# HGRN operands stored crosswise, and the modulation matmuls taken out of the attention stretch of a two-layer trunk kernel

## The chip, the cores and the metric

The kernel runs on one core of one Trainium2 chip. The metric is device time in microseconds (us) of one execution. It was run three times: 2095.54, 2097.5 and 2103.86 us, median 2097.5.

## The reference, cut to what matters

A step of a trunk of two layers (`DEPTH = 2`) over 512 latent and 128 context tokens, width 1024. Each layer makes six modulation vectors, `silu(c) @ w_mod[l] + b_mod[l]`, split as shift, scale and gate for the mixers (numbers 0, 1, 2) and for the FFN (3, 4, 5). One input projection feeds three mixers that run side by side: differential attention, a gated DeltaNet and HGRN2. An output projection, a gated residual with layer norm, a modulated SwiGLU FFN and a second norm follow.

HGRN2 is the part whose code changes:

```python
def gla_chunked(q, k, v, g, s0):          # per direction, scan over tokens
    attn = einsum('bhntsd,bhnsd->bhnts', q[..., :, None, :] * dec, k)   # dec = exp of summed log forget
    intra = einsum('bhnts,bhnse->bhnte', attn, v)
    ...
        o = intra_n + einsum('bhcd,bhde->bhce', qd_n, S)
        S = S * gl_n[..., None] + einsum('bhcd,bhce->bhde', kd_n, v_n)
```

It runs forwards and backwards over four heads of 64, with key = 1 - forget, and the two directions share q and v.

## The kernel before, in words

Tokens are handled in five tiles of 128 (`NT`, number `LT = 4` is the context). Float32 weights are split in two float32r parts: `raw_unit` (L251) loads up to 512 KB into one of three buffers `raw` (pool `praw`), `unit` (L266) lets ACT round them and DVE subtract, and PE multiplies in three passes. All loads and most stores are issued in order on SP's queue. The Tile framework orders each engine's instructions itself, by the order of the program text and a timeline of its own (`schedule_with_timeline_sim=True`, L1767).

A layer runs in these stages.

- First projections: `proj_bg` (L1265, psum tile `pbg`), then four `proj_B` blocks (L1247, `pbq`). `gate_out` (L1240) lets ACT and POOL make a gate and stores it (`gsc`) from a single buffer. In layer 0 they run from 42 to about 95 us, in layer 1 from 1053 to about 1115 us, there beside the norm of layer 0's end (`ptf`).
- The delta mixer, interleaved by `run` (L1332) with the other projections, up to about 350 and 1374 us.
- The attention stretch, up to about 524 and 1551 us. `run` takes turns: one attention query tile (L1187), then, once the delta is over (`open_h`, L1432), two draws of `mods` (L1387), one draw of `hgrn` (L690) and one of `delta_T`. `mods` makes the vectors 3, 4 and 2, folds the first norm's weights into 4 and 3 (`affine`, L506, through the DRAM tile `modrow`), and in layer 0 makes vector 1 of layer 1.
- Output projection (`pop`), with two draws of `mods_late` (L1395) in each of the last five steps: vector 5, and in layer 0 vector 0 of layer 1. Then the FFN (`pfa`, `pfb`, `pfc`, `pfd`, `pfo`); after its first part `affine` folds vectors 1 and 0 of layer 1 (L1677).

`modulation` (L466) takes for each vector eight raw tiles; each is multiplied by four matmuls of 32 columns into psum tile `psm` (the profile shows two records for a float32 matmul, so 8 records a tile). DVE adds the bias (`ms`), and two loads and two stores per vector go over SP. It yields four times per vector.

`hgrn_local` (L579) works with direction 0 on partitions 0 to 63 and direction 1 on 64 to 127. For each token tile, `hq` holds q for both directions, `hK` the keys, `hf` the forget gates. The opening (L605) makes keys on DVE, multiplies keys and queries on PE, masks the diagonal into `haD` on DVE and multiplies q by f on POOL. Then seven levels n = 1, 2, ..., 64 follow, with one draw each for all five tiles. Below 64, in each direction the blocks of the one parity act as queries and of the other as keys: ACT copies the active query blocks of both directions into a tile with zeros elsewhere (`hqm`, L623), eight matmuls of 128 rows by 64 columns per tile (`diag`, L596) sum both directions over all 128 partitions, and DVE puts the product into `haD` where the mask of the level says so (L624). The zeros keep the other direction out. At n = 64 the product goes to `hf` by ACT. At every level, DVE scales the query blocks of each direction (L646) and POOL the key blocks (L647) by gate products `hT`, which POOL makes in a tree (L650). At the end `key_T` (L654) transposes the keys for the states (`pha`), and `out` (L697) makes outputs.

```python
up, lo = 1 - d, d                                    # L640, in a loop over both directions
tt(V, half(Q, d, up), half(Q, d, up), tb(lo), ALU.mult)
tt(G, half(Kr, d, lo), half(Kr, d, lo), tb(up), ALU.mult)
```

PSUM has eight banks: pairs P1, P2, Q and R. `psum_phase` deals them out: first projections `g=QQ+RR`; in the attention stretch one bank (R1) for modulation and three (P2, P2b, R2) for HGRN.

## Time and profile before

| what | value |
|---|---|
| runs | 2095.54, 2097.5, 2103.86 us |
| profiled execution, its own time | 2094.8 us |
| span of that execution, first to last instruction | 2093.0 us |
| mean granted TensorE clock | 0.956 |
| bytes moved by DMA | 249.36 MB |

The profile is of one execution. Engines: PE is TensorE's matmuls, PEld its weight loads, DVE is VectorE, ACT is ScalarE, POOL is GpSimd, SP issues DMAs. A row names line, engine, operation, `written tile<-read tiles`, shape and count. Most instructions are recorded through helpers (L173 for matmuls, L176 for tensor_tensor), so they are told apart by tile names. Matmuls are pipelined: what a run of them costs is read from the start of one run to the start of the next, not from busy time alone.

### The profile page before, as it was taken

To read this page: it belongs to the slowest core of one execution; us is meant where nothing else is said; L and a number is where in the kernel's file an instruction comes from. 1 tells how busy PE (TensorE), PEld (TensorE's weight loads), DVE (VectorE), ACT (ScalarE), POOL (GpSimd) and SP (SyncE) were. 2 spreads that over 40 slices of the span, in tenths; PEclk is the share of its full clock that TensorE was granted. 3 is DMA by queue.
4 is the path that set the end of the run, shared out by engine and by line. 5 is a ranking of instruction groups with operands and counts; after the bars stand their busy time and mean duration, and the time that the engine had idled before them with its cause. 6 is when DMAs were issued, how large, how long until landed. Compare 5 with 4: busy or idle time off the path is not lost.

```text
span 2093.0 us, 37831 instructions
## 1 busy us (share of the span) xinstructions
PE 1912.6 (91%) x14914; PEld 1676.2 (80%) x14914; DVE 1439.1 (69%) x2516; ACT 792.7 (38%) x1564; POOL 883.5 (42%) x988
## 2 busy tenths in 40 slices
PE   7999997888978999999989999978889789999996
PEld 5988986667758989989989879755677779989895
DVE  5458524897488867667666774359847897667676
ACT  3542322666143334323345323146742434334231
POOL 0375235775042132444246814358632311432445
PEclk7999998898999999999999999989899899999998
DMA  8423225865453323222433331386344233223221
GB/s 282 132 77 122 90 68 140 218 195 196 146 164 94 109 81 101 68 84 76 127 121 109 123 116 56 101 192 201 125 158 135 83 109 91 71 81 101 71 77 75
DMA packets 243400, 249.36 MB, mean 119 GB/s; under 512 B 19371, under 2 KB 190359, under 8 KB 243223
## 3 DMA queue, kind: packets, MB, share of 16 engines
q1 hardware_dynamic: 240630, 245.11, 38.4%
q8 instruction: 118, 1.93, 0.4%
q10 hardware_dynamic: 2592, 1.84, 0.3%
q14 instruction: 60, 0.48, 0.1%
HBM read 218.72 MB, written 28.18 MB: 118 GB/s over the span
## 4 chain that ended last, share of the span: by engine, by line
PE 26%; DVE 10%; POOL 5%; DMA 3%; issue 3%; ACT 2%; SPq 1%; POOLq 0%; ACTq 0%; DVEq 0%
PE pfo L173 6%; PE pfd L173 3%; PE pfc L173 3%; PE pfa L173 3%; PE pop L173 3%; PE pfb L173 1%; PE pci L173 1%; DVE hl L176 1%; DVE hq L176 1%; PE pcf L173 1%; POOL r L176 1%; PE pbq L173 1%; PE ph L173 1%; DVE fs L176 1%; DMA avf<-vsc 1%
## 5 line engine op out<-in xcount | busy, mean ns | idle before, releaser
L176 DVE TENSOR_TENSOR hl<-raw,hl 128x1024 fp32r<-128x1024 f32 (+1 forms) x210 | 279.6, 1335 | 92.1 <-ACT hl L273 74.2
L173 PE MATMUL pfo<-hl,ha 128*128 128x512 f32 x1320 | 312.8, 395 | 1.6 <-ACT hl L273 0.8
L173 PEld LDWEIGHTS pfo<-hl,ha 128*128 128x128 f32 x1320 | 246.1, 187 | 60.6 <-DVE ha L176 1.6
L176 POOL TENSOR_TENSOR r<-r,ft 128x512 f32<-128x512 f32 x96 | 142.8, 1506 | 245.2 <-DVE ft L176 244.4
L176 POOL TENSOR_TENSOR t<-raw 128x512 f32<-128x512 f32 x44 | 65.7, 1493 | 336.6 <-DMA raw<-in_w_ffn_in_dram 168.3
L273 ACT CAST hl<-raw 128x1024 fp32r<-128x1024 f32 (+2 forms) x122 | 125.9, 1036 | 152.4 <-DMA raw<-in_w_ffn_out_dram 47.8
L173 PE MATMUL pfc<-sx,hl 128*128 128x320 f32 x1056 | 173.4, 312 | 9.8 <-ACT hl L1550 7.2
L173 PE MATMUL pfa<-xT,hl 128*128 128x320 f32 x1056 | 172.7, 313 | 4.7 <-DVE hl L176 3.0
L173 PEld LDWEIGHTS pfc<-sx,hl 128*128 128x128 f32 x1056 | 161.5, 190 | 13.5 <-ACT hl L1550 7.8
L1550 ACT CAST hl<-raw 128x1024 fp32r<-128x1024 f32 x88 | 92.0, 1051 | 204.4 <-PE pfo L173 105.7
L173 PEld LDWEIGHTS pfa<-xT,hl 128*128 128x128 f32 x1056 | 161.0, 191 | 8.0 <-DVE hl L176 3.8
L173 PE MATMUL paq<-xT,hl 128*128 128x320 f32 x768 | 123.8, 318 | 1.4 <-ACT az L1238 1.4
L173 PE MATMUL pop<-hl,xT 128*128 128x512 f32 x480 | 122.4, 407 | 0.0
L173 PEld LDWEIGHTS paq<-xT,hl 128*128 128x128 f32 x768 | 116.1, 191 | 4.5 <-ACT az L1238 2.1
L173 PEld LDWEIGHTS pop<-hl,xT 128*128 128x128 f32 x480 | 89.5, 193 | 25.2 <-issue 6.8
L176 DVE TENSOR_TENSOR ft<-pfo,lg 128x512 f32<-128x512 f32 x96 | 63.8, 683 | 54.6 <-PE pfo L173 44.1
L176 POOL TENSOR_TENSOR hK<-hK,hT 64x256 f32<-64x256 f32 x120 | 87.6, 730 | 29.9 <-PE ph L173 23.2
L176 DVE TENSOR_TENSOR t<-raw,t 128x512 f32<-128x512 f32 x88 | 73.9, 840 | 35.7 <-POOL t L176 35.6
L173 PE MATMUL pfd<-xT,h 128*128 128x320 f32 x528 | 85.2, 310 | 10.0 <-DVE u L176 10.0
L173 PE MATMUL pbq<-xT,hl 128*128 128x320 f32 x576 | 89.7, 312 | 1.0 <-DVE hl L176 0.4
L173 PE MATMUL pfb<-sx,hl 128*128 128x320 f32 x528 | 88.7, 310 | 0.6 <-DVE hl L176 0.6
L173 PEld LDWEIGHTS pfd<-xT,h 128*128 128x128 f32 x528 | 79.0, 188 | 11.6 <-issue 8.9
(409 smaller groups left out, 4206.1 us busy)
## 6 DMA issues: line engine op xcount, KB each, us to landing
raw<-in_w_ffn_in_dram SPq DMA_DIRECT2D x96, 512.0 KB
raw<-in_w_mod_dram SPq DMA_DIRECT2D x80, 512.0 KB
raw<-in_w_in_dram SPq DMA_DIRECT2D x56, 512.0 KB
raw<-in_w_ffn_out_dram SPq DMA_DIRECT2D x44, 512.0 KB
pc<-in_w_mod_dram SPq DMA_DIRECT2D x8, 1024.0 KB
raw<-in_w_out_dram SPq DMA_DIRECT2D x16, 512.0 KB
qksc<-az SPq DMA_DIRECT2D x16, 320.0 KB
qkhi<-azs SPq DMA_DIRECT2D x16, 256.0 KB
```

The costliest lines, as they stand in the source:

```text
L173: nc.tensor.matmul(out, lhsT, rhs, start=start, stop=stop, **kw)
L176: return eng.tensor_tensor(out, a, b, op)
L273: A.copy(hl[:, 0, :kt * n], raw[:, :kt * n])
L1550: A.copy(tile_[:, 0, :n], raw)
```

## The change

HGRN's operands are stored crosswise. A tile `x` holds in its lower partitions the queries of direction 0 and in its upper the keys of direction 1; a tile `y` holds the keys of direction 0 below and the queries of direction 1 above. So at a level one parity of blocks of `x` is scaled for both directions in one instruction of 128 partitions, and the other parity of `y` in another. `x` is scaled by DVE for token tiles 0, 2 and 4 and by POOL for 1 and 3, `y` by POOL. The products of the two directions are formed apart, by matmuls of 64 rows and 64 columns, twice as many, into a psum bank each, and two masks pick from them. The copies into `hqm` and their zeroed tiles are gone; q is loaded a third time for 64 partitions.

The modulation vectors 3, 4 and 2 of a layer, with their `affine`, are drawn in its first projections, three draws ahead of each `proj_B`. Vector 1 of layer 1 joins 5 and 0 at the end of layer 0, where draws go on in the FFN's steps.

```diff
-    m = [((rc // (2 * b)) == (tc // (2 * b))) & ((rc // b) != (tc // b)) for b in (1, 2, 4, 8, 16, 32)]
+        m += [blk & (rc // b < tc // b), blk & (rc // b > tc // b)]
...
-    hmask = cp.tile([P, 6 * 64], U8, name="hmask")
+    hmask = cp.tile([P, 12 * 64], U8, name="hmask")
+    for i in range(3):
+        S.dma_start(hmf, constm[:, cs_])
+        V.tensor_copy(hmask[:, cs_], hmf)
...
-        for d in range(2):
-            S.dma_start(q5[ds_], cqs[l].rearrange("(h j) t -> j h t", j=64))
+        for sl, t5 in ((LO, x5), (HI, x5), (HI, y5)):
+            S.dma_start(t5[sl], cqs[l].rearrange("(h j) t -> j h t", j=64))
...
+            X[tau] = dict(x=x, y=y, f=f, v=v, kq=((y[LO], x[LO]), (x[HI], y[HI])), T=T, aD=aD, Tv=f, To=0)
...
-            tt(G, x["Q"], x["q"], x["f"], ALU.mult)
+            for k, sl in ((kf, LO), (kb, HI)):
+                A.copy(k, kt[sl])
+            for q, sl in ((qf, LO), (qb, HI)):
+                tt(G, q, q, f[sl], ALU.mult)
...
-                    Qm = hqm[i][tau % len(hqm[i])]
-                        A.copy(half(Qm, d, 1 - d), half(Q, d, 1 - d))
-                    V.copy_predicated(x["aD"], bc(hmask[:, i * 64:(i + 1) * 64], 1, 4),
-                                      diag(x, Qm, f"ph{n}_{l}_{tau}"))
+                    pv = [psS("h", f"ph{n}_{d}_{l}_{tau}")[:, :256].rearrange("p (h t) -> p h t", t=64) for d in range(2)]
+                    for h, d, c_, cs in chunks():
+                        k, q = x["kq"][d]
+                        mm(pv[d][cs, h, :], k[:, h, cs], q[:, h, cs])
+                    for d in range(2):
+                        V.copy_predicated(x["aD"], bc(hmask[:, (2 * i + d) * 64:(2 * i + d + 1) * 64], 1, 4), pv[d])
...
-                    tt(V, half(Q, d, up), half(Q, d, up), tb(lo), ALU.mult)
-                    tt(G, half(Kr, d, lo), half(Kr, d, lo), tb(up), ALU.mult)
+                def scaled(eng, ap, u):
+                    y = ap.rearrange("p h (b u n) -> p h b u n", u=2, n=n)[:, :, :, u, :]
+                    tt(eng, y, y, Tp[:, :, :, 1 - u].unsqueeze(3).to_broadcast([P, 4, nb, n]), ALU.mult)
+                scaled(G if tau % 2 else V, x["x"], 1)
+                scaled(G, x["y"], 0)
...
+            for src, sl in ((x["y"], LO), (x["x"], HI)):
+                for h in range(4):
+                    nc.tensor.transpose(pk[:, h, :], src[:, h, :], ident)
+                A.copy(kn[:, :, sl], pk[:, :, sl])
+            A.copy(x["x"][HI], x["y"][HI])
...
-        psum_phase(g=QQ + RR, n=PP1, d1=PP2)
+        psum_phase(g=QQ + RR[:1], m=RR[1:], n=PP1, d1=PP2)
+        def mods():
+            yield from modulation(l, (3, 4, 2))
+            affine(l, 4, 3, (l, 0), praw, "raw", 3)
...
         for i in range(4):
+            for _ in range(3):
+                next(early_m, 0)
             proj_B(l, i, xT, cv, dp)
+        for _ in early_m:
+            pass
...
             if l + 1 < DEPTH:
-                yield from modulation(l + 1, (0,))
+                yield from modulation(l + 1, (0, 1))
+                affine(l + 1, 1, 0, (l, 1), praw, "raw", 3)
...
-            psum_phase(d1=["P2"], m=["P2b"], d2_dc_as=["Q", "R"], pt_po=PP1)
+            psum_phase(d1=PP2, d2_dc_as=["Q", "R"], pt_po=PP1)
...
-            psum_phase(**{"as": ["Q"], "m": ["R1"], "h": PP2 + ["R2"], "pt_po": PP1})
-            return [(mods(), TURNS[l][3]), (hgrn(l, hp, hqm, xT, held["f5"]), TURNS[l][4]), (delta_T(), 1)]
+            psum_phase(**{"as": ["Q"], "h": PP2 + RR, "pt_po": PP1})
+            return [(hgrn(l, hp, xT, held["f5"]), TURNS[l][4]), (delta_T(), 1)]
...
             for f in range(f0, f1):
+                next(late_m, 0)
                 end = pair_b(f, f - f0)
...
-            if part == 0 and l + 1 < DEPTH:
-                affine(l + 1, 1, 0, (l, 1), praw, "raw", 3)
```

## Rows read from the trace of the kernel before

**Rows 1.** The page's first part: busy time of each engine, its share, instructions.

```profile
PE 1912.6 (91%) x14914; PEld 1676.2 (80%) x14914; DVE 1439.1 (69%) x2516; ACT 792.7 (38%) x1564; POOL 883.5 (42%) x988
```

**Rows 2.** Busy times by stretch; the header names the columns.

```profile
core 0: us, PE busy (x) PEld busy (x) DVE busy (x) ACT busy (x) POOL busy (x), PEclk, DMA share, GB/s
42.00:95.00 53.00, 52.45 (x362) 52.00 (x364) 27.94 (x58) 28.19 (x51) 12.63 (x19) 0.95 0.53 148
380.00:478.00 98.00, 83.27 (x1076) 58.15 (x1071) 91.45 (x198) 64.11 (x193) 77.67 (x122) 0.91 0.66 206
...
1053.00:1127.00 74.00, 68.96 (x482) 66.71 (x483) 49.17 (x69) 39.30 (x67) 39.48 (x44) 0.95 0.40 126
1418.00:1517.00 99.00, 80.70 (x984) 59.66 (x985) 91.63 (x197) 66.49 (x192) 73.27 (x108) 0.90 0.49 152
```

**Rows 3.** Instruction groups of DVE, 380 to 478 us; ends with busy, mean ns.

```profile
L176 DVE TENSOR_TENSOR hq<-hq,hT 64x256 f32<-64x256 f32 x58 | 33.3, 577 | 1.2 <-ACT hqm L623 0.2
L624 DVE COPY_PREDICATED haD<-hmask,ph 128x256 f32<-128x256 uint8 x30 | 12.8, 438 | 0.2
...
L176 DVE TENSOR_TENSOR hq<-hq,hf 64x256 f32<-64x256 f32 x10 | 7.1, 709 | 0.2
...
L176 DVE TENSOR_TENSOR ms<-psm,mbias 128x256 f32<-128x256 f32 x3 | 1.2, 406 | 0.0
```

**Rows 4.** Instruction groups of DVE, 1418 to 1517 us, layer 1.

```profile
L176 DVE TENSOR_TENSOR hq<-hq,hT 64x256 f32<-64x256 f32 x60 | 33.6, 562 | 1.5 <-PE ph L173 0.5
...
L176 DVE TENSOR_TENSOR hq<-hq,hf 64x256 f32<-64x256 f32 x9 | 7.2, 800 | 0.2
```

**Rows 5.** Instructions on tile hq, 380 to 478 us: min/median/max ns.

```profile
L176 DVE TENSOR_TENSOR hq<-hq,hT x58: 399/424/1365, 387.8 to 476.9; 64x256 f32<-64x256 f32 x58
```

**Rows 6.** Instruction groups of POOL, 380 to 478 us.

```profile
L176 POOL TENSOR_TENSOR hK<-hK,hT 64x256 f32<-64x256 f32 x58 | 41.9, 723 | 10.8 <-PE ph L173 7.8
L176 POOL TENSOR_TENSOR hK<-hK,hf 64x256 f32<-64x256 f32 x10 | 9.9, 991 | 3.8 <-PE ph L173 3.3
L176 POOL TENSOR_TENSOR hq<-hq,hf 128x512 f32<-128x512 f32 x5 | 7.5, 1505 | 2.0 <-PE ph L173 2.0
```

**Rows 7.** Instruction groups of ACT, 380 to 478 us.

```profile
L623 ACT COPY hqm<-hq 64x256 f32<-64x256 f32 x60 | 24.0, 410 | 13.5 <-PE ph L173 10.3 <-DVE hq L176 2.5
```

**Rows 8.** PE in order of time, layer 0's HGRN: start, length, what.

```profile
422.83 0.69 PE L173 MATMUL ph<-hqm,hK 128*64 128x64 f32 x16
423.44 0.49 PE L173 MATMUL pas_p<-aks,aqs 64*128 64x128 f32 x4
```

**Rows 9.** PE in order of time, a delta solve.

```profile
219.54 0.40 PE L173 MATMUL pdx<-Y,WT 64*64 64x64 f32 x8
219.78 0.40 PE L173 MATMUL pdx<-Y,dwT 64*64 64x64 f32 x8
```

**Rows 10.** What PE waited for, 380 to 478 us.

```profile
PE psm L173 <- DMA raw<-in_w_mod_dram: 5.3, 2, 4.4
```

**Rows 11.** PE in order of time: modulation in layer 0's output projection, and at 385 us.

```profile
562.60 0.64 PE L173 MATMUL psm<-raw,cm 128*32 128x256 f32 x8
563.17 0.97 PE L173 MATMUL pop<-hl,xT 128*128 128x512 f32 x3
...
384.98 1.50 PE L173 MATMUL psm<-raw,cm 128*32 128x256 f32 x24
```

**Rows 12.** PE in order of time, layer 0's first projections.

```profile
71.45 9.99 PE L173 MATMUL pbq<-xT,hl 128*128 128x320 f32 x67
```

**Rows 13.** SP's queue in order of time: modulation's DMAs at 588, 591 and 401 us.

```profile
588.07 1.11 SPq L482 DMA_DIRECT2D modrow<-ms  x2
...
591.19 8.01 SPq L254 DMA_DIRECT2D raw<-in_w_mod_dram  x5
...
401.39 7.55 SPq L254 DMA_DIRECT2D raw<-in_w_mod_dram  x4
```

**Rows 14.** What PE waited for, 1051 to 1127 us: us in total, times, longest.

```profile
PE ptf L500 <- POOL xmf L176: 5.4, 5, 2.4
```

More of the change, by code (lines that the diff above doesn't have):

```diff
@@ L101, in _const_arrays @@
         cols.append(a)
-    m = [((rc // (2 * b)) == (tc // (2 * b))) & ((rc // b) != (tc // b)) for b in (1, 2, 4, 8, 16, 32)]
+    m = []
+    for b in (1, 2, 4, 8, 16, 32):
+        blk = (rc // (2 * b)) == (tc // (2 * b))
+        m += [blk & (rc // b < tc // b), blk & (rc // b > tc // b)]
     _CONST["f"] = np.concatenate(cols, 1)
@@ L589, in hgrn_local, with chunks @@
             n_ = f"{l}_{tau}"
-            q, f, v = q5[:, :, tsl], f5[:, :, tsl], v5[:, tau]
-            Kr = hp.tile([P, 4, P], F32, tag="hK", bufs=NT, name=f"hK{n_}")
+            x, y, f, v = x5[:, :, tsl], y5[:, :, tsl], f5[:, :, tsl], v5[:, tau]
             T = hp.tile([P, 4, P], F32, tag="hT", bufs=NT, name=f"hT{n_}")
             aD = hp.tile([P, 4, 64], F32, tag="haD", bufs=NT, name=f"haD{n_}")
-            X[tau] = dict(q=q, f=f, v=v, Q=q, K=Kr, T=T, aD=aD, Tv=f, To=0)
-        def diag(x, rhs, nm):
-            ps = psS("h", nm)
+            X[tau] = dict(x=x, y=y, f=f, v=v, kq=((y[LO], x[LO]), (x[HI], y[HI])), T=T, aD=aD, Tv=f, To=0)
+        def chunks():
+            for h in range(4):
+                for d in range(2):
+                    for c_ in range(2):
+                        yield h, d, c_, slice(64 * c_, 64 * c_ + 64)
+        for tau in taus:
+            x = X[tau]
+            f, (kf, qf), (kb, qb) = x["f"], *x["kq"]
+            kt = hp.tile([P, 4, P], F32, tag="hk0", bufs=2, name=f"hk0{l}_{tau}")
+            V.tensor_scalar(kt, f, -1.0, 1.0, ALU.mult, ALU.add)
+            ps = psS("h", f"ph0_{l}_{tau}")
             pv = ps[:, :256].rearrange("p (h t) -> p h t", t=64)
@@ L654, in key_T @@
         def key_T(tau):
-            ps = psS("h", f"phk{l}_{tau}")
-            pk = ps.rearrange("p (j t) -> p j t", t=P)
-            for h in range(4):
-                nc.tensor.transpose(pk[:, h, :], X[tau]["K"][:, h, :], ident)
+            x = X[tau]
             kn = hp.tile([P, 4, P], F32, tag="hkn", bufs=2, name=f"hkn{l}_{tau}")
-            A.copy(kn, pk)
+            for src, sl in ((x["y"], LO), (x["x"], HI)):
+                pk = psS("h", f"phk{sl.start}_{l}_{tau}").rearrange("p (j t) -> p j t", t=P)
+                for h in range(4):
+                    nc.tensor.transpose(pk[:, h, :], src[:, h, :], ident)
+                A.copy(kn[:, :, sl], pk[:, :, sl])
+            A.copy(x["x"][HI], x["y"][HI])
             return kn
@@ L671, in hgrn_local @@
             A.copy(Ab, pa)
[L672 removed]
+            st[tau] = (x["x"], x["Tv"][:, :, 0], Ab, x["aT"], x["v"])
             kn = nxt
@@ L688, in head_norm_out, with hgrn @@
         return o.rearrange("p h d -> p (h d)")
-    def hgrn(l, hp, hqm, xT, f5):
+    def hgrn(l, hp, xT, f5):
         ready = []
@@ L713, in turn @@
                 to_T(o, xT, tau, f"pth{l}_{tau}", ((6, 8),), 6, "h")
-        yield from hgrn_local(l, list(range(NT)), hp, st, hqm, f5)
+        yield from hgrn_local(l, list(range(NT)), hp, st, f5)
         for d in range(2):
@@ L1385, in attn @@
             flush(l, 0)
-        def mods():
-            yield from modulation(l, (3, 4, 2))
-            yield
-            affine(l, 4, 3, (l, 0), praw, "raw", 3)
-            yield
-            if l + 1 < DEPTH:
-                yield from modulation(l + 1, (1,))
         def mods_late():
@@ L1438, in open_h @@
             held["H"], hp = pool(f"H{l}", sB)
-            hqm = [[hp.tile([P, 4, P], F32, name=f"hqm{l}_{i}_{j}") for j in range(2 if i < NQ2[l] else 1)]
-                   for i in range(6)]
-            for t_ in hqm:
-                for q_ in t_:
-                    G.memset(q_, 0.0)
             psum_banks(True)
-            psum_phase(**{"as": ["Q"], "m": ["R1"], "h": PP2 + ["R2"], "pt_po": PP1})
-            return [(mods(), TURNS[l][3]), (hgrn(l, hp, hqm, xT, held["f5"]), TURNS[l][4]), (delta_T(), 1)]
+            psum_phase(**{"as": ["Q"], "h": PP2 + RR, "pt_po": PP1})
+            return [(hgrn(l, hp, xT, held["f5"]), TURNS[l][4]), (delta_T(), 1)]
         tp, over = None, []
```

40 lines of the change are left out of this document (14 added, 26 removed).

## The prediction

> **What bounds the kernel now.** The first part of the page says that PE is busy for 1912.6 us of a span of 2093.0 and DVE for 1439.1 [rows 1]. That is a mean over stages with different limits, so the busy times were read next by stretch. The change touches three kinds. In a layer's first projections PE is busy for 52.45 of 53.00 us (layer 0) and 68.96 of 74.00 (layer 1), while DVE has half its time free: here any new matmul is paid for. In the HGRN part of the attention stretch it is the other way round: DVE is busy for 91.45 of 98.00 us and 91.63 of 99.00, PE for 83.27 and 80.70, POOL for 77.67 and 73.27 [rows 2]. So there a piece of DVE work is worth its time, and a matmul is worth something only where PE keeps others waiting. The profile thus asks one question: the change takes work from a stretch that DVE bounds, and puts modulation into stretches that PE bounds. What does DVE give back, and what does PE charge?
>
> **HGRN on DVE.** A level n below 64 of one token tile now costs DVE two scalings of 64 partitions and one predicated copy; a layer has 60 scalings by hT, 10 by hf and 30 copies. In layer 0 that is 60 x 0.577 + 10 x 0.709 + 30 x 0.438 = 54.8 us [rows 3]. Afterwards the two directions share one scaling of 128 partitions, and only for token tiles 0, 2 and 4: 21 of them, at 256 elements as before, 18 x 0.577 + 3 x 0.709 = 12.5, and 60 copies, 26.3. That saves 16.0 us. The four sums of modulation with its bias leave too, 4 x 0.406 = 1.6. In layer 1, 54.8 us (60 x 0.562, 10 x 0.800, the copies alike) becomes 38.8, and three sums leave: 17.2 us [rows 4].
>
> These 0.577 us are a mean; the median of the same group is 0.424 and its longest 1.365 [rows 5], so something holds DVE up in many of them. GPSIMD Engine Reference of the Trainium skill (Key points) says that GpSimd shares its SBUF interfaces with VectorE and contends with instructions of two SBUF inputs. By that rule the 21 scalings left could run at the median, which would make the sum 21 x 0.153 = 3.2 us a layer better, 2102 in place of 2108. POOL stays as full as before, so I keep the mean.
>
> **HGRN on POOL.** Before: 60 x 0.723 + 10 x 0.991 + 5 x 1.505 = 60.8 us. Afterwards POOL scales 35 blocks of y and, for tiles 1 and 3, 14 of x: 42 x 0.723 + 7 x 0.991 = 37.3. The opening product with f is done twice on 64 partitions, and 64x256 costs half of 128x512 [rows 6], so partitions save nothing: 10 x 1.505 = 15.1. Sum 52.4, 8.4 less, but 7.5 us more of it stand at the front, where the next level's scalings queue behind them on POOL. The opening and level 1 together have 3 fewer scalings of 0.991, so the front grows by some 4.5 us of POOL work while DVE's gain there is about 3: I take the front two turns as no faster. The ends of that cost are nothing and 7.5 us.
>
> **HGRN on ACT and PE.** The masked copies go, 60 x 0.410 = 24.6 us. The row is of 256 elements [rows 7]. Against them stand 10 key copies of 512 elements and, at the end of each tile, a key copy more and one of 512, at most 15 x 0.82 + 5 x 0.41 = 14.4 us; ACT, busy for 64.11 of the 98, isn't near its limit. Each level of a tile issues 32 matmul records on quarter arrays instead of 16 on half arrays. The 16 took 0.61 us from start to next start [rows 8]; eight quarter-array records of the delta solve follow one another in 0.24 [rows 9], so 32 take 0.94, 10 us more a layer. The upper end is twice 0.61. I take 0.94, the same tile form, and it lies beside DVE's work: a level of five tiles is then 4.7 us of PE against 10 x 0.438 + 3 x 0.577 = 6.1 of DVE.
>
> **What the stretch gains.** Five levels from n = 2 save 1.85 us of DVE each, n = 64 saves 4.0, the sums 1.6: 14.9 us, and at DVE's share of 0.93 16 us. From it go 2 us for the four extra transposes and copies per tile at the end, on the way to the states. Layer 0: 14 us less. Layer 1, with three vectors, 13. The 5.3 us in which PE waited for modulation weights here [rows 10] are inside, not added: DVE was busy through most of them.
>
> **First projections.** Three vectors are 24 weight tiles of 512 KB. Eight records set between other matmuls hold PE for 0.57 us; 24 in a row took 1.50, so each further eight add 0.43 [rows 11]. At 0.57 that is 13.7 us a layer, and PE has no room in layer 0. The tile form changes from 128x128 to 128x32 and back at each draw: TensorEngine Tiling of the Trainium skill (Key Properties) says that a change of tiling mode drains TensorE. With two tiles drawn at a time the rule would make it 12 x (0.57 + 0.43) = 12.0, which is 3.4 us less over both layers, 2105; I keep 0.57, since the planner may split the draws.
>
> The weights share three buffers with the projections. One step (a qkv block and six modulation tiles) is 48 x 0.149 + 6 x 0.57 = 10.6 us on PE [rows 11, 12], and seven loads at 1.60 us (five in 8.01 us [rows 13]) take 11.2. So loads run just behind PE: 0.6 us a step, 2.4 us. Each vector also issues four small DMAs on SP and the affine twelve, at 0.55 us of issue time each [rows 13], 13 us of SP in all; they and the weights that wait for a buffer now stand ahead of the projections' gate stores, for which ACT's next gate waits. With SP free otherwise I count 0.6 for it: 3 us in layer 0. Layer 1 loses the same 13.7 and 2 us to loads, but PE waited 5.4 us for the norm here [rows 14]; early draws may fill 2. Together 16.7 and 13.7 us more.
>
> **The layer's end.** Layer 0 draws one more vector, 8 x 0.57 = 4.6 us on PE, and four of its loads stand on SP ahead of the second gate's weights: 6.4 us of queue, of which the matmuls cover about half, so 3 us more. Layer 1 is unchanged. The mask is loaded once in three pieces beside other loads: nothing; without that cover 1 us. The memsets that leave lie in a wait for hf: nothing. Fourth banks for HGRN and one fewer for the projections: nothing, as evacuation is short beside a 3.6 us half; bounds 2 us each way.
>
> **Sum.** -14 - 13 + 16.7 + 13.7 + 7.6 = +11. The profiled execution took 2094.8 us, so 2105.8 by it; the median of the runs is 2097.5, 2.7 above it, which gives **2108**. About 0.5%, 10.5 us, is what a measurement of this kernel can tell from no change, so this lies at its edge.
>
> **Rivals.** (1) DVE's share holds everywhere and PE's gaps take modulation. All the DVE work comes off at its share, 17.6/0.933 + 17.2/0.926 = 37.5 us, and the charge is only PE's clean time, 13.7 + (13.7 - 5.4) + 4.6 = 26.6: 11 us faster, 2086. It decides if POOL's ten opening products don't hold level 1 back. For it: DVE is the fullest engine in both layers; against: POOL was nearly as full in the opening. Chance 0.2. (2) The three weight buffers become the bound in the first projections. In the attention stretch four such loads took 7.55 us, 1.89 each [rows 13]; at that, a step is 13.2 us against 10.6, 10.5 us a layer in place of 3 and 2, and the end loses 3 more: +30, 2127. Chance 0.2. (3) Quarter-array matmuls run at the old rate, 1.22 us for 32; PE then paces DVE and half of the 27 us is not had: +24, 2121. Chance 0.1. (4) The planner orders engines by its own timeline, so the vectors may slip behind the projections, into the delta stage that PE also fills, or the loads go out ahead; the time would be near 2100. Chance 0.05.
>
> **How the numbers follow.** The forecast has 0.45. Half of rival 1 and a tail of the forecast are faster by over 0.5%: 0.16. The rest of rival 1, somewhat under half of the forecast and rival 4 lie within: 0.34. The rest is slower: 0.50. The range reaches from rival 1 to rival 2, 2086 to 2127; the forecast's own is 2099 to 2118, from the unknown costs above.
>
> **What would show it.** Right: the HGRN part shortens by some 14 us, DVE has 60 predicated copies and 21 scalings in it, no psm; 32 records of ph take about 0.9 us; the first projections lengthen by 14 to 17 us with PE still full. Wrong: PE idle there for raw over 5 us (rival 2), the HGRN part shorter by 18 or more (rival 1), or DVE waiting for ph (rival 3).

## The result, and the profile after

The changed kernel took **2169.47 us** (median of 4 runs, 2168.64 to 2172.52) against 2097.78 for the kernel before on the same chip: a ratio of 1.0348, 95% interval 1.033 to 1.0365. It is slower, as forecast, but by 72 us where 10 were forecast, and far outside the range. The profiled execution took 2169.2 us with a span of 2167.1 (2093.0 before) at a mean granted clock of 0.937 (0.956).

The page's first part, for [rows 1]. In the changed file the matmul helper is L175, the tensor-tensor helper L178, a weight load L256 and its cast L275.

```profile
PE 1968.2 (91%) x15914; PEld 1726.7 (80%) x15914; DVE 1409.5 (65%) x2480; ACT 767.9 (35%) x1486; POOL 854.4 (39%) x939
```

PE's share is the same 91%: the page alone shows nothing of a lost 74 us. The starts of four matmul groups in PE's order of time cut the span: the first `pbg` (gate projections), `paq` (delta), `pas` (attention), `pop` (output projection) of each layer. A little delta work lies among the first projections, but in every run the last projection matmul ends within 0.2 us of the first `paq`, so the boundary between them is clean.

| us | before | after | difference | forecast |
|---|---|---|---|---|
| up to the first `pbg` | 42.1 | 40.8 | -1.3 | 0 |
| layer 0: first projections | 72.9 | 129.6 | **+56.7** | +16.7 |
| delta | 235.7 | 234.9 | -0.8 | 0 |
| attention stretch | 173.7 | 158.4 | -15.3 | -14 |
| rest of the layer | 531.9 | 542.5 | +10.6 | +7.6 |
| layer 1: first projections | 71.1 | 103.6 | **+32.5** | +13.7 |
| delta | 245.4 | 242.9 | -2.5 | 0 |
| attention stretch | 178.3 | 165.7 | -12.7 | -13 |
| rest | 541.9 | 548.7 | +6.8 | 0 |

Busy times of layer 0's first projections, its HGRN part, and the same two of layer 1, for [rows 2]:

```profile
core 0: us, PE busy (x) PEld busy (x) DVE busy (x) ACT busy (x) POOL busy (x), PEclk, DMA share, GB/s
40.80:170.40 129.60, 102.78 (x689) 86.14 (x690) 37.91 (x89) 40.56 (x71) 22.12 (x32) 0.81 0.56 169
430.40:522.40 92.00, 84.94 (x1369) 69.41 (x1369) 78.59 (x180) 47.44 (x144) 68.02 (x110) 0.86 0.31 79
1106.20:1209.80 103.60, 87.49 (x638) 74.42 (x637) 50.21 (x70) 39.26 (x63) 34.37 (x38) 0.88 0.64 197
1483.10:1578.40 95.30, 87.20 (x1369) 72.80 (x1370) 79.13 (x178) 48.33 (x145) 67.92 (x110) 0.86 0.27 71
```

Before the change, layer 0's first projections up to the first `paq` were:

```profile
42.10:115.00 72.90, 72.45 (x496) 70.26 (x497) 34.79 (x79) 38.65 (x70) 21.30 (x32) 0.94 0.43 122
```

In the first projections PE is no longer full: idle for 26.8 of 129.6 us, at a granted clock of 0.81. In the HGRN part PE now holds 84.9 of 92.0 us and DVE 78.6: the bound has changed sides. Two views say what PE lacks in layer 0's first projections, and what SP's queue does meanwhile (us in total, times, longest):

```profile
PE psm L175 <- DMA raw<-in_w_mod_dram: 12.4, 6, 3.4
PE pbq L175 <- ACT hl L275: 6.8, 3, 3.5
PE pbg L175 <- ACT dls L430: 4.9, 1, 4.9
```

```profile
SPq L256 <- PE psm L175: 30.7, 14, 8.4
SPq L256 <- DVE hl L178: 15.9, 6, 7.4
...
SPq L424 <- DMA hmf<-in_constm_dram: 4.2, 1, 4.2
```

One step of it, in PE's order of time and then in SP's:

```profile
99.06 7.42 PE L175 MATMUL pbq<-xT,hl 128*128 128x320 f32 x44
106.41 1.50 PE L175 MATMUL psm<-raw,cm 128*32 128x256 f32 x24
111.22 1.08 PE L175 MATMUL psm<-raw,cm 128*32 128x256 f32 x8 [3.31 <-DMA raw<-in_w_mod_dram]
112.48 1.08 PE L175 MATMUL psm<-raw,cm 128*32 128x256 f32 x8 [0.18 <-DMA raw<-in_w_mod_dram]
115.21 1.44 PE L175 MATMUL pbq<-xT,hl 128*128 128x320 f32 x4 [1.64 <-ACT hl L275]
116.57 1.08 PE L175 MATMUL psm<-raw,cm 128*32 128x256 f32 x8
117.58 8.29 PE L175 MATMUL pbq<-xT,hl 128*128 128x320 f32 x44
```

```profile
90.61 17.30 SPq L256 DMA_DIRECT2D raw<-in_w_mod_dram  x6
108.01 0.38 SPq L256 DMA_DIRECT2D raw<-in_w_in_dram  x1
...
112.35 14.96 SPq L256 DMA_DIRECT2D raw<-in_w_mod_dram  x6
```

While PE does a block (99.06 to 106.41), three modulation tiles fill the ring of three buffers, and SP, which waits for PE to free one, issues no load from 99.20 to 107.11. When PE comes to the three it does them in 1.50 us, and then waits for the others, and for the block's own weights, which SP issues only at 108.01, behind the sixth tile. From block to block a step is 18.5 us. Seven loads of 1.60 us and the 7.4 us of the block are 18.6: the two run nearly one after the other. The DMA share is 0.41 during the block and 0.77 from its end to the next.

### The profile page after: what moved, and what is told of

It is laid out like the page before. It is cut to its first block, busy times and chain, and to the rows that moved or that the text cites. A ratio compares the mean times of both kernels' runs of the same rounds, so it can differ in the third digit from the quotient of the medians.

```text
span 2167.1 us, 39706 instructions
## 1 busy us (share of the span) xinstructions
PE 1968.2 (91%) x15914; PEld 1726.7 (80%) x15914; DVE 1409.5 (65%) x2480; ACT 767.9 (35%) x1486; POOL 854.4 (39%) x939
## 4 chain that ended last, share of the span: by engine, by line
PE 56%; DVE 14%; DMA 6%; POOL 6%; issue 4%; ACT 3%; SPq 1%; POOLq 0%; DVEq 0%; ACTq 0%
PE pfo L175 12%; PE pfa L175 6%; PE pfd L175 6%; PE pfc L175 6%; PE pop L175 5%; PE pfb L175 3%; PE pci L175 2%; PE ph L175 2%; PE pcf L175 2%; DVE hl L178 2%; PE pao L175 2%; DMA raw<-in_w_ffn_in_dram 1%; PE pbq L175 1%; POOL r L178 1%; DMA raw<-in_w_mod_dram 1%
## 5 line engine op out<-in xcount | busy, mean ns | idle before, releaser
L178 DVE TENSOR_TENSOR hl<-raw,hl 128x1024 fp32r<-128x1024 f32 (+1 forms) x210 | 282.6, 1350 | 101.2 <-ACT hl L275 83.0
L175 PE MATMUL pfo<-hl,ha 128*128 128x512 f32 x1320 | 314.8, 396 | 0.1
L175 PEld LDWEIGHTS pfo<-hl,ha 128*128 128x128 f32 x1320 | 246.8, 188 | 58.8 <-DVE ft L178 1.0
L178 POOL TENSOR_TENSOR r<-r,ft 128x512 f32<-128x512 f32 x96 | 141.8, 1497 | 246.9 <-DVE ft L178 246.5
L178 POOL TENSOR_TENSOR t<-raw 128x512 f32<-128x512 f32 x44 | 69.8, 1586 | 344.4 <-DMA raw<-in_w_ffn_in_dram 166.9
L275 ACT CAST hl<-raw 128x1024 fp32r<-128x1024 f32 (+2 forms) x122 | 125.7, 1035 | 172.3 <-DMA raw<-in_w_ffn_out_dram 48.6
L175 PE MATMUL pfa<-xT,hl 128*128 128x320 f32 x1056 | 178.5, 319 | 7.7 <-ACT hl L1559 5.1
L175 PE MATMUL pfc<-sx,hl 128*128 128x320 f32 x1056 | 175.1, 315 | 10.9 <-ACT hl L1559 9.4
L175 PEld LDWEIGHTS pfa<-xT,hl 128*128 128x128 f32 x1056 | 165.7, 196 | 12.6 <-ACT hl L1559 6.3
L175 PEld LDWEIGHTS pfc<-sx,hl 128*128 128x128 f32 x1056 | 163.4, 192 | 14.3 <-ACT hl L1559 10.4
L1559 ACT CAST hl<-raw 128x1024 fp32r<-128x1024 f32 x88 | 92.1, 1051 | 217.9 <-PE pfo L175 103.6
L175 PE MATMUL paq<-xT,hl 128*128 128x320 f32 x768 | 123.2, 317 | 0.6 <-ACT az L1249 0.6
L175 PEld LDWEIGHTS paq<-xT,hl 128*128 128x128 f32 x768 | 115.8, 190 | 3.4 <-ACT az L1249 1.2
L175 PE MATMUL pop<-hl,xT 128*128 128x512 f32 x480 | 118.0, 401 | 0.0
L175 PE MATMUL pbq<-xT,hl 128*128 128x320 f32 x576 | 104.7, 344 | 10.4 <-ACT hl L275 10.3
L175 PEld LDWEIGHTS pbq<-xT,hl 128*128 128x128 f32 x576 | 97.7, 215 | 20.0 <-ACT hl L275 13.9
L175 PEld LDWEIGHTS pop<-hl,xT 128*128 128x128 f32 x480 | 89.0, 190 | 23.7 <-issue 4.9
L178 DVE TENSOR_TENSOR t<-raw,t 128x512 f32<-128x512 f32 x88 | 77.1, 876 | 43.1 <-POOL t L178 42.9
L178 DVE TENSOR_TENSOR ft<-pfo,lg 128x512 f32<-128x512 f32 x96 | 63.8, 683 | 53.8 <-PE pfo L175 46.2
L175 PE MATMUL pfb<-sx,hl 128*128 128x320 f32 x528 | 89.8, 312 | 1.7 <-DVE hl L178 1.7
L175 PE MATMUL psm<-raw,cm 128*32 128x256 f32 x640 | 57.3, 444 | 35.4 <-DMA raw<-in_w_mod_dram 32.0
L175 PE MATMUL pfd<-xT,h 128*128 128x320 f32 x528 | 85.0, 310 | 4.9 <-DVE u L178 4.9
```

The source lines that it names most:

```text
L175: nc.tensor.matmul(out, lhsT, rhs, start=start, stop=stop, **kw)
L178: return eng.tensor_tensor(out, a, b, op)
L275: A.copy(hl[:, 0, :kt * n], raw[:, :kt * n])
L1559: A.copy(tile_[:, 0, :n], raw)
```

## The experiments

All were timed beside the kernel before, whose median was 2092.0 to 2094.4 us there; the first two rows of the table are the runs of the result, where it was 2097.8. So two rows are compared more safely by their ratios to it than by their microseconds. Stages are cut as above: P is the first projections, up to the first `paq`, "att" the attention stretch, "rest" what follows up to the next layer or the end. The expectations quote P and delta as one sum (308.6, 364.5, 316.5).

| kernel | us | P 0 | delta 0 | att 0 | rest 0 | P 1 | delta 1 | att 1 | rest 1 |
|---|---|---|---|---|---|---|---|---|---|
| before | 2097.8 | 72.9 | 235.7 | 173.7 | 531.9 | 71.1 | 245.4 | 178.3 | 541.9 |
| changed | 2169.5 | 129.6 | 234.9 | 158.4 | 542.5 | 103.6 | 242.9 | 165.7 | 548.7 |
| storage alone | 2115.0 | 80.9 | 235.7 | 186.4 | 531.2 | 74.1 | 243.1 | 174.9 | 543.2 |
| the same, mask in one piece | 2104.5 | 77.9 | 230.2 | 179.2 | 535.5 | 73.2 | 238.9 | 186.9 | 542.3 |
| move alone | 2184.6 | 121.7 | 227.3 | 174.1 | 545.4 | 104.0 | 242.3 | 177.8 | 551.4 |
| changed, finer draws | 2132.0 | 116.6 | 227.9 | 167.6 | 539.9 | 100.5 | 233.8 | 162.1 | 545.7 |
| no early loads | 2112.0 | 88.5 | 237.6 | 168.6 | 542.9 | 74.8 | 243.8 | 166.1 | 550.3 |
| early loads, few matmuls | 2132.7 | 111.4 | 229.8 | 167.8 | 542.4 | 90.3 | 244.0 | 166.0 | 541.3 |
| own buffers, layer 0 | 2133.6 | 95.6 | 227.0 | 166.5 | 541.4 | 104.5 | 241.5 | 176.3 | 541.3 |
| mask in one piece | 2158.9 | 121.1 | 227.2 | 169.0 | 538.8 | 104.3 | 240.6 | 171.9 | 540.1 |
| affine back | 2156.1 | 130.0 | 229.8 | 158.5 | 540.8 | 99.9 | 243.7 | 167.6 | 541.2 |
| three banks | 2182.1 | 128.9 | 232.0 | 167.8 | 544.5 | 104.4 | 240.1 | 178.9 | 543.4 |
| storage, few matmuls | 2115.1 | 83.0 | 241.1 | 184.5 | 532.8 | 73.6 | 251.6 | 171.8 | 543.6 |
| storage, matmuls without loads | 2106.6 | 78.8 | 235.2 | 182.3 | 532.8 | 74.1 | 246.6 | 170.6 | 543.3 |
| ring, mask, draws | 2135.1 | 96.6 | 235.5 | 169.3 | 540.6 | 100.4 | 229.8 | 167.6 | 549.0 |
| all mended | 2136.4 | 97.9 | 229.3 | 180.2 | 541.1 | 90.3 | 235.3 | 174.3 | 551.1 |

P repeats well: layer 1's is 103.6 to 104.5 us in the five kernels whose code for it is the same (changed, move alone, own buffers, mask, three banks). The other stages do not. The seven kernels with the changed kernel's attention code (changed, finer draws, no early loads, few matmuls, own buffers, mask, and ring, mask, draws) took 158.4 to 169.3 us for it in layer 0 and 162.1 to 176.3 in layer 1. Layer 0's delta stage, the same code in all, took 227.0 to 241.1, and layer 1's rest, the same in most, 540.1 to 551.4. So outside P one stage of one profile tells nothing below some 10 us.

**1. The storage alone.** Modulation and both affine calls go back to where the kernel before has them:

```
-        psum_phase(g=QQ + RR[:1], m=RR[1:], n=PP1, d1=PP2)
+        psum_phase(g=QQ + RR, n=PP1, d1=PP2)
-            return [(hgrn(l, hp, xT, held["f5"]), TURNS[l][4]), (delta_T(), 1)]
+            return [(mods(), TURNS[l][3]), (hgrn(l, hp, xT, held["f5"]), TURNS[l][4]), (delta_T(), 1)]
```

> Crosswise storage alone; modulation and its two affine calls stay where the kernel before has them. Ring theory (three shared weight buffers make loads and matmuls take turns in the first projections, and all of the loss is there): the HGRN part of each attention stretch is still shorter, by 8 to 13 us a layer because modulation is still in it, the first projections are as before but for up to 5 us of the mask's chain, so 2072 to 2090 us. Rival (the new storage costs as much elsewhere as it saves: more matmul records, POOL's longer front, key copies): 2095 to 2105 us.

Measured 2115.0 us, ratio 1.0097 (1.0063 to 1.0131). Both theories fell: the storage alone makes the kernel some 1% slower. Layer 0's attention stretch grew by 12.7 us, layer 1's fell by 3.5. HGRN has three PSUM banks here, as modulation still holds the fourth.

**2. The move alone**, put into the kernel before, with its storage and mask:

```
+            for _ in range(3):
+                next(early_m, 0)
             proj_B(l, i, xT, cv, dp)
```

> The modulation's move alone, with the HGRN storage and mask of the kernel before. Ring theory: layer 0's first projections lengthen by about 50 us (55 less the mask's 5), layer 1's by about 32, the end of layer 0 by about 8, and the attention stretches win at most 4 us each: 2170 to 2190 us, so slower than the changed kernel itself (2169.5). Rival (the two halves disturb each other, for instance the mask's pieces ahead of the weights cause most of the 55 us): under 2150 us.

Measured 2184.6, ratio 1.0433 (1.0403 to 1.0462), inside the ring theory's bounds. The attention stretches win nothing, +0.4 and -0.6 us, though HGRN gets the fourth PSUM bank here too.

**3. Finer draws.** One draw, two tiles, at a time:

```
         for h in range(2):
+            if HOOK:
+                next(HOOK[0], 0)
```

> The changed kernel with the same loads, buffers and matmuls, but the early modulation is drawn in pairs of weight tiles spread over the step: one draw after each token tile of the gate projections from the second on and one before each half of each qkv block, where the changed kernel draws three in a row ahead of each block. Ring theory: a ring of three is enough when at most two modulation tiles stand between two uses of projection weights, so loads run beside matmuls again; the first projections lose 15 to 30 us in layer 0 and 12 to 20 in layer 1 in place of 55 and 32: 2110 to 2140 us, and PE's waits for modulation weights and for the projections' own weights fall by more than half. Rival (PE's price for 32-column matmuls set between others, with a switch of tile form at each draw, is the cost): twice as many switches, so no better: 2165 to 2185 us.

Measured 2132.0, ratio 1.0186 (1.0165 to 1.0207). The total is inside the ring theory's bounds, but not by its mechanism: P falls by 13.0 us in layer 0 and 3.1 in layer 1, so the first projections still lose 43.7 and 29.4 us, where 15 to 30 and 12 to 20 were expected (35.9 and 17.7 with delta). Of the other gains 16.1 us lie in the delta stages, whose code is the same. PE goes to modulation's matmuls or back 42 times in layer 0's P in place of 22, and 38 times in layer 1's in place of 24, and neither became longer, so these changes are not the main cost. In layer 0's P, PE's waits for modulation weights fell from 12.4 to 1.2 us, those for the projections' own weights did not (6.8 and 6.9). The longest is for the last block's weights; SP's queue shows them behind the affine's small transfers:

```profile
119.39 1.07 SPq L490 DMA_DIRECT2D modrow<-ms  x2
120.84 2.70 SPq L529 DMA_DIRECT2D modrow<-aff  x4
123.65 1.91 SPq L256 DMA_DIRECT2D raw<-in_w_in_dram  x3
```

```profile
128.60 1.43 PE L175 MATMUL pbq<-xT,hl 128*128 128x320 f32 x4 [6.48 <-ACT hl L275]
```

**4. No early loads.** The 24 tiles a layer are not loaded; the matmuls stay in number and form.

```
-                raw, _ = raw_unit(w_mod[l][k * P:(k + 1) * P, i * D:(i + 1) * D].unsqueeze(1), 1, D)
+                raw = None if noload else raw_unit(w_mod[l][k * P:(k + 1) * P, i * D:(i + 1) * D].unsqueeze(1), 1, D)[0]
```

> The changed kernel without the 24 weight loads of the three early vectors in each layer: their matmuls multiply a tile that is in SBUF anyway, so these three vectors are not computed from the modulation weights; number, form and place of the matmuls stay. Ring theory: what is left is PE's price, some 14 us a layer, and the mask's 5 us, in place of 55 and 32, so 2169.5 - 36 - 18 = about 2115 us (2100 to 2125). Rival (PE's price for the matmuls and their switches): all of the loss stays, 2155 to 2170 us.

Measured 2112.0, ratio 1.0084 (1.0063 to 1.0105). The first projections of the two layers, columns as above:

```profile
40.70:129.30 88.60, 86.14 (x626) 76.26 (x627) 36.03 (x89) 44.03 (x74) 22.21 (x32) 0.92 0.39 106
1078.40:1153.20 74.80, 72.62 (x577) 66.52 (x575) 48.09 (x67) 36.02 (x60) 32.76 (x39) 1.00 0.35 106
```

The total is inside the ring theory's bounds. Without the loads PE is full and its clock is back at 0.92 and 1.00, and P falls by 41.1 and 28.8 us. Not all of that is the loads', since the place of the matmuls did not stay: 64 of the 192 records of layer 0's early vectors now run before the first `pbg`, where the changed kernel has none, and 94 of layer 1's, where it has 32. By the 0.57 us of eight records [rows 11], these 64 and 62 more are an estimated 4.6 and 4.4 us. So some 36 of the 56.7 us lost in layer 0 are the loads', and some 24 of the 32.5 in layer 1.

**5. Six buffers of their own** for layer 0's early modulation:

```
-        raw = praw.tile([P, 1024], F32, tag="raw", name="raw")
+        raw = own.tile([P, 1024], F32, tag="mraw", bufs=6, name="mraw") if own else praw.tile([P, 1024], F32, tag="raw", name="raw")
```

> The changed kernel, in layer 0's first projections with six weight buffers for modulation alone beside the three shared ones; layer 1 as it was. Ring theory (three buffers: loads wait for PE to free one): all six tiles of a step load while PE does the block before, so layer 0's first projections and delta stage fall by 20 to 30 us of their 364.5: 2140 to 2150. Rival (the in-order queue of SP is enough to make them take turns: a block's own weights still stand behind six modulation loads): a fall of under 8 us.

Measured 2133.6, ratio 1.02 (1.0181 to 1.022): 36 us back by nothing but buffers. Layer 0's P falls by 34.0 us with all 192 records in it; with delta it is 41.9, more than the 20 to 30 expected.

```profile
40.40:136.10 95.70, 91.50 (x689) 77.98 (x690) 38.03 (x91) 42.85 (x73) 22.39 (x32) 0.92 0.72 230
```

The same loads now move at 230 GB/s in place of 169, beside a PE that is busy for 91.5 of 95.7 us. So neither DMA bandwidth nor the matmuls were the limit.

**6. All early loads, few matmuls.** A tile that nothing reads is free once it has landed:

```
-                for g in range(4):
+                for g in range(4 if not nomm or k == 0 else 0):
```

> The changed kernel with all loads of the early vectors, of which only the first of eight tiles is multiplied (so these three vectors are not computed from all their weights); a tile that nothing reads is free for the next load as soon as it has landed, so this takes the hold of PE on the ring away and leaves the 24 transfers a layer. Ring theory (the hold is what costs): the first projections come near those of the kernel without the loads, 2095 to 2120 us. Rival (24 transfers of 512 KB beside the projections' own are simply too much for the DMA engines there): 2135 us or more.

Measured 2132.7, ratio 1.0196 (1.0176 to 1.0216): between the two theories. P falls by 18.2 and 13.3 us. PE's hold on the ring is gone; the ring's three places, now freed by landings, and the in-order queue are left:

```profile
PE pbq L175 <- ACT hl L275: 17.5, 3, 8.8
```

```profile
SPq L256 <- DMA raw<-in_w_mod_dram: 25.2, 15, 5.4
```

SP waits for landed tiles, and PE for block weights that stand behind them. So the loss has both parts, the ring and the queue; buffers of their own, run 5, mend both in layer 0. That the queue then need not stop is the reading of these waits; no run changed the queue alone.

**7. The mask in one piece**, through a weights buffer; by itself, and with the storage alone:

```
-    for i in range(3):
-        hmf = cp.tile([P, 256], F32, tag="dl", name=f"hmf{i}")
...
+    hmf = praw.tile([P, 1024], F32, tag="raw", name="hmf")
```

> The changed kernel with the mask loaded in one piece into a weights buffer, in place of three pieces through the small buffer that the lambda vectors share. Mask theory (each piece waits for the copy of the one before, and the lambdas, the scalar that ACT makes of them and with it the first gate evacuation wait for the last): layer 0's first projections shorten by 5 to 8 us, 2161 to 2165. Rival (the chain is hidden behind the weight loads): 2168 to 2171.

> Crosswise storage alone with the mask in one piece. Mask theory: layer 0's first projections are back at 73 to 75 us in place of 80.9, and the whole is 7 to 10 us below the 2115.0 of crosswise storage alone: 2105 to 2108. What is left above the kernel before is the attention stretch that PE now bounds. Rival (the mask's pieces cost only beside the moved weights): 2112 to 2117.

Measured 2158.9, ratio 1.0316 (1.0288 to 1.0345), and 2104.5, ratio 1.0065 (1.0038 to 1.0092): 10.6 and 10.5 us by the medians, 6.7 in both by the ratios, whose intervals overlap with those of the two kernels without this edit. Layer 0's P shows it more firmly: 8.5 us less in the one (129.6 to 121.1) and 3.0 in the other (80.9 to 77.9, where 73 to 75 was expected). The three pieces shared one buffer with the lambdas, so the lambdas' exponential on ACT, ahead of the first gate evacuation, came late: the 4.9 us of PE above, a wait that is gone in the first of these runs.

**8. What makes the storage pay.** Three runs take the attention stretch apart: the storage alone with one in eight of that stretch's modulation matmuls, by the edit of run 6; with all of them on a tile already in SBUF, without the loads, by that of run 4; and the changed kernel with three PSUM banks for HGRN in place of four.

```
-            psum_phase(**{"as": ["Q"], "h": PP2 + RR, "pt_po": PP1})
+            psum_phase(**{"as": ["Q"], "h": PP2 + ["R2"], "pt_po": PP1})
```

> Crosswise storage alone, as in the run before it (2115.0 us, layer 0's attention stretch 186.4 us with PE busy for 109.8 of the HGRN part's 116), but of the eight weight tiles of each vector of the attention stretch only the first is multiplied; all are loaded, so these vectors are not computed from all their weights. Two-bounds theory (with the old storage DVE bounds the stretch, with the new one PE does, because its HGRN matmuls take 14 us more; so the matmuls of modulation cost nothing there before and their full time now): some 22 us of PE leave layer 0's stretch and 16 layer 1's, and the stretches fall to about 165 and 165: 2080 to 2092 us. Rival (it is the fourth PSUM bank for HGRN, or the weights' transfers, that the move of modulation frees): both stay as they are here, 2105 to 2115.

> Crosswise storage alone with modulation left in the attention stretch, whose matmuls are all issued but multiply a tile that is in SBUF anyway: none of that stretch's weight tiles is loaded (so the vectors made there are not computed from the modulation weights). It is the counterpart of the run with all loads and an eighth of the matmuls, which gained nothing (2115.1 against 2115.0). Transfer theory (512 KB tiles stand on SP and on the DMA engines among the attention's own loads, late HGRN inputs and keys follow): layer 0's delta and attention stages together fall from 422 us to 395 to 402, as without modulation, and the whole to 2080 to 2092. Rival (PE: with the new storage its matmuls bound the stretch, whether or not there are loads): 2108 to 2118. Rival (the fourth PSUM bank): the same 2108 to 2118, but then the run with three banks loses what this one does not win.

> The changed kernel with three PSUM banks for HGRN's matmuls in the attention stretch, as with modulation in place, one bank left unused. Bank theory (the fourth bank is what makes the new storage pay): delta and attention stages of layer 0 lengthen by 15 us or more, layer 1's by 8 or more, 2190 us. Rival (the bank is worth nothing much, as the prediction had it, 2 us each way): 2165 to 2174.

Measured 2115.1 (1.0114, 1.0076 to 1.0152), 2106.6 (1.0064, 1.0043 to 1.0085) and 2182.1 (1.0416, 1.0388 to 1.0444). Taking out matmuls alone wins nothing. Taking out loads alone wins 8 us by the medians, which the overlapping intervals don't tell from nothing. The bank is worth 12.6 us by the medians, clear of noise in the total (the changed kernel's interval ends at 1.0365); the stretches are 9.4 and 13.2 longer, but 167.8 lies within what the changed attention code takes with four banks, and 178.9 is 2.6 above it. Each theory expected one cause, and none has it alone. Whole attention stretches suggest why, columns as above. Layer 0 of before, storage alone, move alone, changed, and the storage with few matmuls, one fence each:

```profile
350.80:524.40 173.60, 140.11 (x1468) 107.86 (x1467) 142.46 (x307) 105.83 (x312) 116.46 (x192) 0.88 0.70 207
```

```profile
357.50:543.90 186.40, 160.46 (x1971) 125.52 (x1969) 127.55 (x286) 94.14 (x279) 96.91 (x168) 0.87 0.64 180
```

```profile
389.30:563.40 174.10, 129.94 (x1213) 110.58 (x1212) 146.46 (x313) 106.96 (x314) 118.67 (x197) 0.80 0.42 117
```

```profile
405.30:563.70 158.40, 133.97 (x1713) 112.99 (x1712) 123.28 (x281) 91.28 (x272) 100.31 (x168) 0.89 0.44 114
```

```profile
365.10:549.70 184.60, 151.48 (x1749) 127.65 (x1747) 123.33 (x289) 92.71 (x278) 97.43 (x168) 0.80 0.56 155
```

In each, the stretch is 1.16 to 1.22 times its fuller engine: DVE's 142.5 before and 146.5 with the move alone, PE's 160.5 with the storage alone, 151.5 with few matmuls, 134.0 after. The storage takes 15 us off DVE and puts 20 on PE; the move takes modulation off PE. Each alone leaves one engine as full as before, or fuller; both together relieve both. That this sets the stretch is argued from these shares and not shown by a run of its own. With few matmuls some 22 us of modulation left PE, yet it kept 151.5 us: the granted clock was 0.80 in place of 0.87, and HGRN's own `ph` took 49.8 us in place of 44.7.

**9. The affine calls back in the attention stretch**, by themselves, then with all repairs together (buffers, mask, layer 1's finer draws, no added draws at layer 1's end), then without the affine's move and the last:

```
             yield from modulation(l, (3, 4, 2))
-            affine(l, 4, 3, (l, 0), praw, "raw", 3)
+
+        def aff():
+            yield
+            affine(l, 4, 3, (l, 0), praw, "raw", 3)
+            yield
...
-                next(late_m, 0)
+                if l + 1 < DEPTH:
+                    next(late_m, 0)
```

> The changed kernel with the affine call of each layer back in the attention stretch, where the kernel before has it; the three vectors stay in the first projections. Theory (sixteen small transfers and their DVE work are late for the projections' last weights, and harmless in the stretch): 2162 to 2168. Rival (in the stretch they cost 10 us or more a layer, as the mended kernel's 180.2 us in place of 166.5 suggests): 2175 to 2190.

> The changed kernel with what the earlier runs point to put together: six weight buffers of their own for modulation in layer 0's first projections, the finer draws in layer 1's (SBUF has no room for the buffers there), the mask in one piece, the affine calls in the attention stretch as before, and no additional draws in layer 1's end. Ring theory: layer 0's first projections and delta stage come within 8 us of before (308.6), layer 1's within 18 (316.5), the attention stretches keep their 12 to 15 us, layer 0's end its 10 us more: 2092 to 2106 us, no better than the kernel before within what can be told. Rival (part of the loss in the first projections is PE's own): 2110 to 2125.

> The changed kernel with layer 0's six own weight buffers, the mask in one piece and layer 1's finer draws, but with the affine calls in the first projections and the draws of layer 1's end as in the changed kernel: the mended kernel (2136.4) without its two other edits. Theory that the terms add and that the affine's place in the attention stretch spoiled the mended kernel: 2133.6 of the run with own buffers, less 8 to 10 for the mask, less 8 to 12 for layer 1's draws: 2110 to 2118. Rival (terms don't add: what the first projections give up comes back as lower clock and another order of the attention stretch): 2128 to 2140.

Measured 2156.1 (1.03, 1.0271 to 1.0329), 2136.4 (1.0202, 1.0168 to 1.0236) and 2135.1 (1.019, 1.0153 to 1.0228). The first lies below both of its expectations, the second above both, the third within its rival's. By itself the affine's place is worth 13 us by the medians and 10 by the ratios, but P shows only part of it: 3.7 us in layer 1 and nothing in layer 0 (129.6 and 130.0). Beside the finer draws it is worth 10.1 us of layer 1's P (100.4 to 90.3, the last two runs, which differ in the affine's place and in layer 1's end). The repairs do not add up: with the mask, layer 1's draws and the affine mended too, the kernel is where six buffers alone put it. Layer 1's P and delta are better by 16 to 21 us, and layer 0's P and delta, its attention stretch and layer 1's rest give it back. In the mended kernel's layer 0 stretch PE was busy for 150.3 us at a granted clock of 0.79, where the changed kernel's was busy for 134.0 with as many matmuls, at 0.89:

```profile
368.44:548.60 180.16, 150.28 (x1719) 127.90 (x1717) 127.49 (x286) 93.52 (x279) 104.52 (x171) 0.79 0.34 86
```

SP's order is another there too: HGRN's inputs (`hx<-cqs`, at 397.57) stand behind the second head's loads, where the changed kernel issues them (at 420.09) ahead of them. That the planner's order, or the clock, gives the gains back fits, but no run changed either alone, so it stays open. No version beat the kernel before.

## Why the prediction was wrong

**Direction right, size wrong.** The chance of slower was 0.50; the time lies 42 us beyond the range's end, and the first projections' +56.7 and +32.5, where +16.7 and +13.7 were forecast, make 58.8 of the 61 us by which it was missed.

**The first projections are the failed step:** "So loads run just behind PE: 0.6 us a step, 2.4 us." It set 11.2 us of loads against 10.6 of PE as if each had a buffer to go on with. With three buffers and one queue in order, loads and blocks take turns: 18.5 us a step. The loads cost some 36 us in layer 0 and 24 in layer 1 (run 4), and buffers alone give 34.0 back in layer 0 (run 5), where 2.4 and 2 stood in the sum. Rival 2 had the right place, and its sign showed (PE idle for `raw` for 12.4 us, over 5), but it priced the three buffers by a slower load, 13.2 us a step, and not by the turn-taking. The profile before could have told: [rows 13] shows loads that are held, 7.55 us for four, and SP's waits from 401 to 409.5 us say by what, PE's matmuls on the tiles that fill the ring:

```profile
SPq L254 <- PE psm L173: 8.1, 4, 3.4
```

That question was not asked.

**PE's price** was right for a tile, and short in total. In run 5 a tile set singly between other matmuls still holds PE for 0.57 us (62.56 to 63.13), but PE's busy time in layer 0's P is 91.5 us against 72.5 before, 19.0 more where 13.7 stood. Modulation's records take 14.3 of it, and the old work 4.7 more, at a clock of 0.92 against 0.94. In layer 1 without loads, P has 98 records, some 12 tiles, and is 3.7 us longer than before, where 12 tiles are 7.0 by the forecast; PE's earlier waits [rows 14] may have taken the rest in. TensorEngine Tiling (Array Packing) of the Trainium skill states (Tiling Modes, Key Properties) that a change of tile form drains TensorE; no run here isolates that, and nearly twice the changes went with a shorter P (run 3).

**"The mask is loaded once in three pieces beside other loads: nothing; without that cover 1 us":** it is 8.5 in layer 0's first projections (run 7). The cover was DMA time; the price was a buffer shared with the lambdas and a chain that ends ahead of PE's first gate.

**The affine on SP**, counted in the 0.6 us of queue for layer 0 and at nothing in layer 1: in layer 1's P it is 3.7 us by itself and 10.1 beside finer draws, in layer 0's none that P shows (run 9).

**The attention stretch, -14 and -13,** came out as -15.3 and -12.7, partly by luck: the six other kernels with the same attention code won 4.4 to 7.2 us in layer 0 and 2.1 to 16.2 in layer 1. The sign that was named did not show: the HGRN part, from the first to the last `ph`, shortened by 6.9 and 3.9 us (98.8 to 91.9, 97.9 to 94.0), and with the move alone, on the old storage, by 12.5 and 13.5, with less attention work between its matmuls (162 and 169 other PE records, against 249 and 239 in the changed kernel). Layer 0's, with the move alone:

```profile
428.50:514.80 86.30, 61.85 (x802) 50.37 (x802) 81.86 (x168) 55.34 (x160) 70.84 (x111) 0.79 0.16 46
```

DVE's work fell as worked out:

```profile
L636 DVE COPY_PREDICATED haD<-hmask,ph 128x256 f32<-128x256 uint8 x60 | 25.2, 437 | 2.5 <-PE ph L175 2.0
...
L178 DVE TENSOR_TENSOR hx<-hx,hT 128x256 f32<-128x256 f32 x18 | 9.5, 526 | 0.6 <-PE ph L175 0.6
```

60 copies and 21 scalings were forecast at 26.3 and 12.5 us; the copies took 25.2 and the 18 of these scalings that use hT 9.5 (526 ns each: a third of the way from the 577 that was kept to the median of 424, where the rule of GPSIMD Engine Reference of the Trainium skill, Key points, would have them). But the storage alone gained nothing, and PE became the fuller engine in it: rival 3's mechanism, given 0.1, though run 8 doesn't show that PE alone set the stretch. The gain came only where modulation's matmuls and loads left, which the sum had put on the other side of the ledger alone. The matmul price was near in total: PE's busy time on `ph` rose by 12.8 us in each layer (30.5 to 43.3 and 32.7 to 45.4), where 10 were forecast. What 32 records take depends on their order. Two 16-record halves of a level, one direction each, from start to next start (the first to `pas_p`, the second to a transpose at 465.24):

```profile
463.60 0.68 PE L175 MATMUL ph<-hy,hx 64*64 64x64 f32 x16 [1.00 <-DVE haD L636]
464.21 0.49 PE L175 MATMUL pas_p<-aks,aqs 64*128 64x128 f32 x4
464.63 0.68 PE L175 MATMUL ph<-hx,hy 64*64 64x64 f32 x16
```

Each half takes 0.61 us, as long as the 16 half-array records of [rows 8]; 32 thus cost 1.22, the upper end, where they come in two halves. Where the two directions alternate, 32 records took 0.63 us to the next start (busy times of instructions on `ph` alone; the last three numbers are as above):

```profile
481.37:482.00 0.63, 0.63 (x32) 0.55 (x32) 0.09 (x1) 0.00 (x0) 1.00 0.10 26
```

TensorEngine Tiling (Array Packing) of the Trainium skill gives 64x64 tiles up to twice the rate for each small dimension (Overview). The alternating records show that factor of two over 128x64, the halves show none.

**"Fourth banks for HGRN ...: nothing; bounds 2 us each way":** 12.6 us (run 8). Trainium Kernel Development and Optimization of the Trainium skill (Best Practices) says that tiling TensorE speeds up the matmuls but not the evacuation of PSUM. With two PSUM tiles for each level in place of one, the 12.6 us fits that, but the traces show it only in part: with three banks DVE's copies waited 5.6 and 10.6 us for `ph` in the two stretches, in place of 2.0 and 6.2.

**Layer 0's rest,** +7.6, came out as +10.6, and +6.9 to +13.5 in the other runs with the late vector. Layer 1's +6.8 is no cost that can be shown: the same code took 540.1 us in another run, less than before.

## What to carry to other kernels

A load stream that is put beside a running one is priced by its buffers and its queue, not by its rate: count how many of its tiles can land while the engine works on something else, and what stands behind them in order. Where two engines are nearly equally full, a change that relieves one and a change that relieves the other may each be worth nothing and together something, so test the pair and its halves. Where a planner reorders the rest, look for a stage that repeats (here the first projections, within 1 us) before a gain of some microseconds is put down to an edit. And a small load in a shared buffer is only free if nothing on the path waits for that buffer's next user.

## What the runs showed that was not expected

PE's granted clock moved with how its work lay. It was 0.94 in layer 0's first projections before, 0.81 when PE waited in each step, and 0.92 again with six buffers or without loads. PE was busy there for 72.5 us before and 102.8 after; of the 30.3 more, 17.8 are modulation's records, and 12.5 are the old work, longer at the lower clock (72.5 x 0.94 / 0.81 is 84.1, and it took 85.0). In the HGRN part a full PE had a low clock in some kernels and not in others: 440 to 460 us of the storage with few matmuls, and 428 to 448 of the mended kernel, against 420 to 440 of the storage alone:

```profile
440.00:460.00 20.00, 20.00 (x263) 16.36 (x261) 14.11 (x37) 6.99 (x24) 8.00 (x15) 0.66 0.68 202
```

```profile
428.00:448.00 20.00, 18.58 (x219) 15.67 (x219) 15.11 (x39) 5.20 (x18) 9.43 (x13) 0.50 0.30 74
```

```profile
420.00:440.00 20.00, 19.76 (x360) 13.93 (x357) 16.36 (x44) 8.59 (x30) 10.01 (x15) 1.00 0.73 215
```

A PE that is busy for 18.6 of 20 us was granted half of full speed, which is the lower of its two levels, 1.2 GHz, throughout. What sets it in this mixture of small matmuls was not tried.
